# A two-layer hybrid decoder trunk on one core: the instruction order of the scheduler's timeline simulation in place of that of its default model

## The chip, the cores and the metric

The kernel runs on one core of a Trainium2 chip. A core has a matrix engine (TensorE, in the rows PE for the multiplications and PEld for the loading of weights), a vector engine (VectorE, DVE), a scalar engine (ScalarE, ACT), a general engine (GpSimd, POOL) and a queue processor that issues most transfers (SyncE, SP). Each engine runs its own list of instructions in the order in which the program holds them; semaphores order the lists against each other. The metric is the device time of one execution in microseconds, the median of several.

## The reference

The reference is a decoder trunk of two layers on 1024 positions of width 1024, in float32. Cut to what matters:

```python
for i in range(DEPTH):                                  # DEPTH = 2
    proj = rmsnorm(h, attn_norm_g[i]) @ w_in[i]         # one projection, split in ten parts
    y_a = mla_group(c_q, c_kv, k_rope, positions, ...)  # latent attention, rotary key
    y_b = fox_group(fox_qkv, fox_f, fox_b_f[i])         # attention with forget gates
    y_c = hgrn2_group(hg_q, hg_f, hg_i, lb_all[i])      # gated linear recurrence
    y_d = s5_group(s5_u, lam, step, b, c, d, w_glu, ..) # complex diagonal scan, then a GLU
    y = concatenate([rmsnorm(y_a), rmsnorm(y_b), rmsnorm(y_c) * sigmoid(hg_g), rmsnorm(y_d)])
    h = h + y @ w_out[i]
    h = h + conv_ffn(rmsnorm(h, ...), w_up[i], conv_w[i], conv_b[i], w_down[i])  # width 2816, conv of 3
    h = h + sigmoid(rmsnorm(h, ...) @ w_ple_gate[i]) * (p[i] @ w_ple[i])
return rmsnorm(h, final_norm_g)
```

Each of the four groups has 256 of the 1024 columns: four heads of 64 in `mla_group`, `fox_group` and `hgrn2_group`, sixteen blocks of 16 channels with 64 complex states in `s5_group`.

## The kernel before

Activations lie with the features on the 128 partitions and the positions along the row, in halves of 512 positions (tag `h`, 72 buffers). Every float32 product is made as three products of a rounded part and a rest: lines 732 to 734 (`mm3`) and 744 to 746 (`mm3_steps`) issue hi·hi, lo·hi and hi·lo for each block of 128 features. A weight therefore comes in three steps, in `wload`: a DMA on the SP queue into `wr` (2 buffers), a cast to the high part on VectorE (line 720, `wx<-wr`), and the rest on GpSimd or another engine (line 103, `wx<-wr,wx`). `wx` has 6 buffers, so three weights with their two parts; a cast must wait until the products with the weight that had the buffers before are done. PSUM is cut into pools of banks (`pf`, `px`, `po`).

A layer runs in stages that the program writes one after the other, the parts of a stage interleaved by `weave` (a table `T` says at which share of the projection each part begins and ends):

- In-projection, S5 and the recurrence (66 to about 420 us in layer 0, 1583 to 1945 in layer 1). `proj` makes `pj` tiles (24 products each for one half of the positions), `proj_tok` the token-major `ptk`. In the rows `pj<-xs,wx 128*68` is the projection `misc` (68 columns: the rotary key and the forget gates); VectorE takes it out of PSUM at line 1643. Beside it run `s5_mats` (matrices `bare`, `baim` on VectorE and `care`, `caim` on GpSimd, by `cmul`, lines 399 to 404: a complex product of 128x128 tiles is six instructions) and `s5_core` for the two halves of the S5 channels: scans `s5z` on VectorE (lines 591 to 615), 48 products `ys` (lines 625 and 628) on TensorE, transposes `yf` (line 641). `s5_glu` then has the products `gl`. The recurrence has `khT`, `psc`, `poh` on TensorE and `kh`, `qz` on VectorE and GpSimd.
- Attention (420 to 744, 1945 to 2260): logits `lg` and `qk`, maxima `pm`, values `po`, woven with the output projection `ob` of the groups that are done; VectorE adds each `ob` tile into the residual `h` (lines 1765 and 1788).
- FFN up (744 to 1185, 2260 to 2710), FFN down (1185 to 1455, 2710 to 2930; `dn` at lines 1521 to 1523), the gated input embedding (`pg`), and at the very end the final norm.

At the start of a layer's use of a norm, `ss` (line 804) sums squares by a product with ones, and the factor of the norm is then made on ScalarE (lines 810 and 811).

The order of the instructions on each engine is not that of the program text. The framework's scheduler walks through all recorded instructions and lays, engine by engine, the recorded instruction with the best priority (the earliest in the text) that its model of the machine takes to be ready: operands written, a buffer of the pool free. That order is then fixed; the same walk gives out the buffers of each pool. The scheduler is switched on where `kernel` opens the context, at line 2007; all work is written in `body`.

## Time and profile before

| | us |
|---|---|
| median of 3 runs | 3096.61 |
| lowest, highest of them | 3095.42, 3107.64 |
| the profiled execution's own time | 3083.79 |
| its span in the trace | 3082.1 |
| TensorE busy in the span | 2798.3 (91%) |
| VectorE busy | 2521.0 (82%) |
| ScalarE, GpSimd busy | 1403.3, 1228.8 |

The profiled execution is 12.8 us under the median of the runs; its span leaves 1.7 us around it. The rows further down are all of this one execution. Times are from the span's start. [...]

### The profile page before, as it was taken

To read this page: it belongs to the slowest core of one execution; us is meant where nothing else is said; L and a number is where in the kernel's file an instruction comes from. 1 tells how busy PE (TensorE), PEld (TensorE's weight loads), DVE (VectorE), ACT (ScalarE), POOL (GpSimd) and SP (SyncE) were. 2 spreads that over 40 slices of the span, in tenths; PEclk is the share of its full clock that TensorE was granted. 3 is DMA by queue.
4 is the path that set the end of the run, shared out by engine and by line. 5 is a ranking of instruction groups with operands and counts; after the bars stand their busy time and mean duration, and the time that the engine had idled before them with its cause. 6 is when DMAs were issued, how large, how long until landed. Compare 5 with 4: busy or idle time off the path is not lost. (4 is left out here: it accounts for less than half of the span.)

```text
span 3082.1 us, 37399 instructions
## 1 busy us (share of the span) xinstructions
PE 2798.3 (91%) x13082; PEld 2229.8 (72%) x13082; DVE 2521.0 (82%) x3572; ACT 1403.3 (46%) x2448; POOL 1228.8 (40%) x1108
## 2 busy tenths in 40 slices
PE   8889898898999999888999888988989999998897
PEld 6767676676788887666887766766767888876766
DVE  7596878769999998888855877878699999979987
ACT  3124445765444443335722353657654444423355
POOL 3653423445422223555544434324453222245554
PEclk9889999899999999999998989999999999999998
DMA  3101021004122225632511010210032222255423
GB/s 124 37 15 35 20 73 60 9 1 151 67 87 87 83 83 174 202 102 79 161 65 35 18 35 21 79 55 1 35 123 82 83 82 82 78 194 176 134 84 127
DMA packets 124812, 249.70 MB, mean 81 GB/s; under 512 B 18896, under 2 KB 21584, under 8 KB 124624
## 3 DMA queue, kind: packets, MB, share of 16 engines
q1 hardware_dynamic: 123184, 246.66, 23.8%
q8 instruction: 103, 1.69, 0.2%
q10 hardware_dynamic: 1440, 0.65, 0.1%
q14 instruction: 85, 0.70, 0.1%
HBM read 197.58 MB, written 48.50 MB: 80 GB/s over the span
## 5 line engine op out<-in xcount | busy, mean ns | idle before, releaser
L103 POOL TENSOR_TENSOR wx<-wr,wx 128x512 fp32r<-128x512 f32 (+1 forms) x200 | 412.1, 2061 | 433.9 <-DVE wx L720 106.1
L1324 PE MATMUL up<-bh,wx 128*128 128x512 f32 x1232 | 483.2, 392 | 12.1 <-ACT wx L1317 12.1
L1325 PE MATMUL up<-bl,wx 128*128 128x512 f32 x1232 | 483.3, 392 | 6.8 <-DVE bl L103 4.0
L1326 PE MATMUL up<-bh,wx 128*128 128x512 f32 x1232 | 483.6, 392 | 6.3 <-DVE wx L103 6.3
L1523 PE MATMUL dn<-g,wx 128*128 128x512 f32 x616 | 252.3, 410 | 49.9 <-POOL wx L103 25.3
L103 POOL TENSOR_TENSOR pl<-pr,ph 128x512 fp32r<-128x512 f32 x144 | 166.2, 1167 | 308.4 <-ACT pr L980 198.1
L1324 PEld LDWEIGHTS up<-bh,wx 128*128 128x128 f32 x1232 | 233.6, 190 | 62.0 <-ACT wx L1317 13.0
L1325 PEld LDWEIGHTS up<-bl,wx 128*128 128x128 f32 x1232 | 233.9, 190 | 57.3 <-DVE bl L103 4.9
L1326 PEld LDWEIGHTS up<-bh,wx 128*128 128x128 f32 x1232 | 233.3, 189 | 56.7 <-DVE wx L103 8.4
L103 POOL TENSOR_TENSOR wx<-wq,wx 128x512 fp32r<-128x512 f32 x44 | 65.1, 1479 | 517.5 <-ACT wx L1317 517.5
L1521 PE MATMUL dn<-g,wx 128*128 128x512 f32 x616 | 249.7, 405 | 15.6 <-ACT p L1532 11.8
L1522 PE MATMUL dn<-g,wx 128*128 128x512 f32 x616 | 248.8, 404 | 6.0 <-DVE g L103 6.0
L744 PE MATMUL pj<-xs,wx 128*128 128x512 f32 (+1 forms) x512 | 213.0, 416 | 18.9 <-ACT xs L771 7.2
L746 PE MATMUL pj<-xs,wx 128*128 128x512 f32 (+1 forms) x512 | 206.7, 404 | 4.7 <-POOL wx L103 4.2
L745 PE MATMUL pj<-xs,wx 128*128 128x512 f32 (+1 forms) x512 | 208.1, 406 | 0.9 <-DVE xs L772 0.9
L1523 PEld LDWEIGHTS dn<-g,wx 128*128 128x128 f32 x616 | 121.0, 196 | 88.0 <-DVE wx L103 31.6
L1440 ACT CAST g<-g 128x512 fp32r<-128x512 f32 x154 | 92.4, 619 | 154.2 <-DVE g L1463 51.7
L1521 PEld LDWEIGHTS dn<-g,wx 128*128 128x128 f32 x616 | 121.1, 197 | 45.3 <-ACT p L1532 12.6
L1335 DVE SCALAR_TENSOR_TENSOR cv<-u,vec,cv 128x1023 f32<-128x1023 f32 x88 | 131.1, 1491 | 25.5 <-ACT cv L1334 25.2
L1522 PEld LDWEIGHTS dn<-g,wx 128*128 128x128 f32 x616 | 120.9, 196 | 32.9 <-DVE g L103 6.8
L1334 ACT ACTIVATE cv<-u,vec 128x1024 f32<-128x1024 f32 x88 | 109.6, 1245 | 71.7 <-DVE u L1349 46.5
L1336 DVE SCALAR_TENSOR_TENSOR cv<-u,vec,cv 128x1022 f32<-128x1022 f32 x88 | 139.1, 1583 | 0.1
(493 smaller groups left out, 7481.0 us busy)
## 6 DMA issues: line engine op xcount, KB each, us to landing
wr<-in_w_down SPq DMA_DIRECT2D x132, 256.0 KB, 3.1
wr<-in_w_up SPq DMA_DIRECT2D x88, 256.0 KB, 2.9
wq<-in_w_up SPq DMA_DIRECT2D x88, 256.0 KB, 3.8
hid<-cv SPq DMA_DIRECT2D x44, 512.0 KB, 3.0
g<-hid SPq DMA_DIRECT2D x88, 256.0 KB, 5.0
wr<-in_w_fm SPq DMA_DIRECT2D x30, 512.0 KB, 3.7
wr<-in_w_pg SPq DMA_DIRECT2D x28, 512.0 KB, 3.6
hdr<-h SPq DMA_DIRECT2D x48, 256.0 KB, 2.0
```

What stands on the lines that cost most here:

```text
L103: eng.tensor_tensor(out, x, hi.bitcast(F32), op=ALU.subtract)
L744: nc.tensor.matmul(out, lhsT=ah, rhs=bh, start=(i == 0), stop=False)
L745: nc.tensor.matmul(out, lhsT=ah, rhs=bl, start=False, stop=False)
L746: nc.tensor.matmul(out, lhsT=al, rhs=bh, start=False, stop=(i == n - 1))
L1324: nc.tensor.matmul(ps, lhsT=ah, rhs=bh, start=k == 0, stop=False)
L1325: nc.tensor.matmul(ps, lhsT=ah, rhs=bl, start=False, stop=False)
L1326: nc.tensor.matmul(ps, lhsT=al, rhs=bh, start=False, stop=k == KD // 2 - 1)
L1335: V.scalar_tensor_tensor(c[:, 1:], u[:, :S - 1], cw[:, 1:2], c[:, 1:], op0=ALU.mult, op1=ALU.add)
L1336: V.scalar_tensor_tensor(c[:, 2:], u[:, :S - 2], cw[:, 0:1], c[:, 2:], op0=ALU.mult, op1=ALU.add)
L1521: nc.tensor.matmul(o, lhsT=ah, rhs=gh, start=f == 0, stop=False)
L1522: nc.tensor.matmul(o, lhsT=ah, rhs=gl, start=False, stop=False)
L1523: nc.tensor.matmul(o, lhsT=al, rhs=gh, start=False, stop=f == H - 1)
```

## The change

```diff
@@ -2004,7 +2004,7 @@
-    with tile.TileContext(nc) as tc:
+    with tile.TileContext(nc, schedule_with_timeline_sim=True) as tc:
         body(tc, *args, out)
```

The keyword gives the scheduler another model to walk by: one that also simulates how the engines and the other shared devices of a core contend, in place of the default one. No operation, tile, size or engine assignment is changed; every instruction of before is there again by name. What changes is the order on each engine, the buffers that follow from it, and the semaphore waits.

On TensorE the FFN up stage stands as before (the same rows at the same places), as does most of the rest behind the attention; in FFN down the third product of a block (line 1523) stands up to 14 rows further back, behind the first two products of the next tiles. The large moves are in the in-projection and attention stages. At three places they read as follows; the number behind a name is the tile's.

TensorE, layer 0, first half of the S5 channels (`ys_1301`, `ys_1302`) and `misc` (`pj_1341`): before, the last `ys` rows and what follows them.

```order
L628 MATMUL ys_1301<-care_779,s5z_1241 128x128
L628 MATMUL ys_1301<-caim_780,s5z_1242 128x128
L625 MATMUL ys_1302<-tz_989,ut_1197 128x128
L628 MATMUL ys_1302<-care_779,s5z_1241 128x128
L628 MATMUL ys_1302<-caim_780,s5z_1242 128x128
L744 MATMUL pj_1341<-xs_114,wx_1337 68x512
L745 MATMUL pj_1341<-xs_114,wx_1337 68x512
L746 MATMUL pj_1341<-xs_114,wx_1338 68x512
```

After, the last rows of the second half of `misc` (`pj_1415`), the first of the next projection (`pj_1506`, a part of the fox queries), and the `ys` rows that come between them.

```order
L744 MATMUL pj_1415<-xs_174,wx_1337 68x512
L745 MATMUL pj_1415<-xs_175,wx_1337 68x512
L746 MATMUL pj_1415<-xs_174,wx_1338 68x512
L744 MATMUL pj_1506<-xs_114,wx_1502 128x512
L745 MATMUL pj_1506<-xs_114,wx_1502 128x512
L746 MATMUL pj_1506<-xs_114,wx_1503 128x512
L628 MATMUL ys_1301<-care_779,s5z_1241 128x128
L628 MATMUL ys_1302<-care_779,s5z_1241 128x128
L744 MATMUL pj_1506<-xs_117,wx_1502 128x512
L745 MATMUL pj_1506<-xs_117,wx_1502 128x512
```

All but two of the 48 `ys` rows have gone behind the 48 rows of `misc`; the projection `fq` runs between and behind them. The same happens in layer 1 (`pj_13909` and `pj_13983` before `ys_13869`).

VectorE at the same place: the S5 scan (lines 610 to 615), the casts of weights (line 720), `misc` (line 1643) and the first of the 24 instructions that make `bare` and `baim`. Before:

```order
L612 TENSOR_TENSOR s5z_1242<-s5z_1238,phr_1087 128x4x127
L613 TENSOR_TENSOR s5z_1241<-s5z_1241,s5z_1240 128x4x127
L615 TENSOR_TENSOR s5z_1242<-s5z_1242,s5z_1239 128x4x127
L720 CAST wx_1717<-wr_1715 128x1024
L1642 TENSOR_TENSOR hq_1200<-pj_1275,rs_340 128x512
L1643 TENSOR_TENSOR misc_1333<-pj_1341,rs_256 68x512
L399 TENSOR_TENSOR s5t_1387<-bb_764,s5v_728 128x128
L400 TENSOR_TENSOR s5t_1388<-bb_764,s5v_728 128x128
```

After:

```order
L610 TENSOR_TENSOR s5z_1241<-s5z_1239,phr_1087 128x4x127
L612 TENSOR_TENSOR s5z_1242<-s5z_1238,phr_1087 128x4x127
L613 TENSOR_TENSOR s5z_1241<-s5z_1241,s5z_1240 128x4x127
L615 TENSOR_TENSOR s5z_1242<-s5z_1242,s5z_1239 128x4x127
L720 CAST wx_1977<-wr_1975 128x1024
L1643 TENSOR_TENSOR misc_1333<-pj_1341,rs_256 68x512
L399 TENSOR_TENSOR s5t_1387<-bb_764,s5v_728 128x128
L400 TENSOR_TENSOR s5t_1388<-bb_764,s5v_728 128x128
```

`misc` stands behind the same scan. The cast `wx_1717` has gone in front of the scan (row 229 of VectorE's list instead of 248) and `wx_1977` has come in front of `misc` (239 instead of 278). Further on two more casts are early: `wx_1983` at row 259 instead of 333, and the weight of the GLU, `wx_2425`, at row 286 instead of 454. The scans of the second half of the S5 channels, in turn, stand 25 to 29 rows further back.

TensorE, layer 0, where the second half of the S5 channels is transposed (`yf_2231`, `yf_2238`), before: the token-major projection (`ptk_2143`, `ptk_2255`) around it.

```order
L733 MATMUL ptk_2143<-wx_1984,xs_135 128x256
L734 MATMUL ptk_2143<-wx_1983,xs_135 128x256
L641 MATMUL yf_2231<-ident,yt_2137 128x128 x4
L641 MATMUL yf_2238<-ident,yt_2138 128x128 x4
L330 MATMUL psc_2245<-qz_2087,g_2082 128x2x64 x4
L732 MATMUL ptk_2255<-wx_1977,xs_142 128x256
L733 MATMUL ptk_2255<-wx_1978,xs_142 128x256
L734 MATMUL ptk_2255<-wx_1977,xs_143 128x256
```

After:

```order
L628 MATMUL ys_2112<-care_1385,s5z_1924 128x128
L628 MATMUL ys_2112<-caim_1386,s5z_1925 128x128
L641 MATMUL yf_2231<-ident,yt_2137 128x128 x4
L641 MATMUL yf_2238<-ident,yt_2138 128x128 x4
L330 MATMUL psc_2245<-qz_2087,g_2082 128x2x64 x4
L330 MATMUL psc_2310<-qz_2106,g_2101 128x2x64 x4
L330 MATMUL psc_2320<-qz_2180,g_2175 128x2x64 x4
L330 MATMUL psc_2384<-qz_2197,g_2192 128x2x64 x4
```

The 48 `ys` rows of the second half stand some 140 to 170 rows further back, directly ahead of `yf`. The 96 `ptk` rows and the 24 rows of the projection `pj_2537` that stood between `yf` and the end of `gl` now stand ahead of `yf`; behind it only `psc`, `poh`, `gl` and 24 rows of `pj_2679` are left, of which 9 stood there before. By the next chunk of the recurrence (`khT_2702`) both orders have done the same set.

At the start of the attention stage the first `ob` row group (`ob_3518`) now stands ahead of the sum of squares `ss_3370`, and VectorE's addition of it (line 1788) ahead of the four instructions of lines 829 and 831 that wait for that norm; 48 `ob` rows instead of 34 stand ahead of the first `lg`, more of them among the next `lg` rows, and the first `pm` (`pm_3626`) stands 60 rows further back. At the program's start the first `ss` stands behind 14 more rows of `pj`.

## Rows read from the trace of the kernel before

**Rows 1.** The page: the span, and the engines' busy time in it.
```profile
span 3082.1 us, 37399 instructions
PE 2798.3 (91%) x13082; PEld 2229.8 (72%) x13082; DVE 2521.0 (82%) x3572; ACT 1403.3 (46%) x2448; POOL 1228.8 (40%) x1108
```
**Rows 2.** Windows of both layers' attention, busy time: PE, PEld, DVE, ACT, POOL, clock, DMA.
```profile
420.00:560.00 140.00, 128.22 (x598) 95.71 (x598) 112.10 (x206) 85.11 (x167) 41.04 (x45) 0.94 0.13 42
560.00:744.00 184.00, 164.36 (x779) 125.09 (x779) 139.28 (x228) 121.84 (x244) 90.75 (x88) 0.96 0.14 50
1945.00:2260.00 315.00, 281.48 (x1334) 211.48 (x1334) 241.73 (x418) 201.38 (x399) 125.87 (x129) 0.96 0.12 41
```
**Rows 3.** Waits of VectorE, whole span: total us, times, longest.
```profile
DVE misc L1643 <- PE pj L746: 41.4, 2, 20.9
```
**Rows 4.** Timeline of VectorE behind that wait, layer 0: start, duration, idle before.
```profile
153.32 0.69 DVE L1643 TENSOR_TENSOR misc<-pj,rs 68x512 f32<-68x512 f32 x1 [20.54 <-PE pj L746]
153.93 0.28 DVE L399 TENSOR_TENSOR s5t<-bb,s5v 128x128 f32<-128x128 f32 x1
```
**Rows 5.** Windows on both sides of the end of that wait.
```profile
128.00:154.00 26.00, 23.02 (x83) 16.33 (x83) 5.46 (x7) 5.12 (x11) 15.13 (x29) 0.67 0.10 31
154.00:222.00 68.00, 53.73 (x364) 45.17 (x363) 65.28 (x174) 19.00 (x43) 32.00 (x53) 0.93 0.06 17
```
**Rows 6.** Waits of TensorE in 60 to 420: one.
```profile
PE ys L628 <- DVE s5z L613: 3.0, 1, 3.0
```
**Rows 7.** Windows of `ys` alone (PE, PEld, ACT, clock): layer 0, layer 1.
```profile
131.00:145.50 14.50, 14.46 (x46) 10.97 (x46) 0.65 (x2) 0.50 0.13 40
1741.70:1749.40 7.70, 7.67 (x48) 5.92 (x48) 0.65 (x2) 1.00 0.01 2
```
**Rows 8.** Groups of VectorE by shape, 78 to 93: busy us, mean ns.
```profile
L403 DVE TENSOR_TENSOR s5t<-bb,s5v 128x128 f32<-128x128 f32 x4 | 2.0, 492 | 0.0
L402 DVE TENSOR_TENSOR s5t<-bb,s5v 128x128 f32<-128x128 f32 x4 | 1.5, 369 | 0.0
```
**Rows 9.** Window of that stretch (all engines), and timeline of GpSimd during VectorE's wait.
```profile
78.00:93.00 15.00, 8.52 (x71) 8.11 (x69) 13.59 (x43) 1.89 (x5) 12.50 (x32) 0.90 0.02 5
...
135.70 0.41 POOL L400 TENSOR_TENSOR s5t<-prm,s5v 128x128 f32<-128x128 f32 x1
```
**Rows 10.** Windows: `yf` to `gl` (all engines), then `ptk` alone and `pj` alone.
```profile
247.40:291.40 44.00, 41.57 (x259) 33.56 (x258) 28.19 (x37) 21.58 (x39) 13.89 (x8) 0.96 0.11 37
...
261.10:264.20 3.10, 3.03 (x24) 2.94 (x24) 0.43 (x2) 1.00 0.00 0
...
123.80:127.60 3.80, 3.80 (x18) 3.00 (x16) 0.68 (x1) 1.00 0.29 116
```
**Rows 11.** Timeline of TensorE at the start of attention, layer 0.
```profile
409.06 1.12 PE L804 MATMUL ss<-sq,ones 128*128 128x512 f32 x2 [1.08 <-DVE sq L796]
...
417.30 0.39 PE L734 MATMUL ob<-yh,wx 128*128 128x512 f32 x1
420.37 0.50 PE L732 MATMUL ob<-yh,wx 128*128 128x512 f32 x1 [2.68 <-DVE ckv L1642]
```
**Rows 12.** Timeline of VectorE there: the first step behind the norm.
```profile
411.61 0.75 DVE L829 SCALAR_TENSOR_TENSOR xn<-yc,vec,rs 128x512 f32<-128x512 f32 x1 [2.60 <-ACT rs L811]
```
**Rows 13.** Timeline of TensorE at the program's start.
```profile
35.59 2.08 PE L804 MATMUL ss<-sq,ones 128*128 128x512 f32 x2 [4.45 <-DVE sq L796]
```
**Rows 14.** Waits of TensorE in FFN down of layer 0, 1185 to 1455.
```profile
PE dn L1523 <- DVE wx L103: 15.8, 11, 3.1
PE dn L1523 <- POOL wx L103: 10.8, 5, 3.3
```
**Rows 15.** Window in FFN down, layer 0.
```profile
1253.00:1322.00 69.00, 54.83 (x218) 43.09 (x219) 66.32 (x69) 25.45 (x47) 37.32 (x24) 0.93 0.52 169
```

## The prediction

> **What bounds the kernel now.** I read the page first. TensorE is busy 2798.3 of 3082.1 us and VectorE 2521.0 [rows 1]: TensorE leads nearly everywhere, and VectorE is close behind it. No operation changes, so the 283.8 us in which TensorE is idle, and the time that it runs at the lower clock level, are all that another order can win; what it can lose has no such limit. The FFN up stage, where both orders are the same, is out of it. That leaves the in-projection stage, attention, FFN down and the start.
>
> Second came the waits of VectorE. One stands out: its instruction for `misc` waits for the `pj` product 41.4 us in two times, once in each layer, 20.9 at the longest, so 20.5 and 20.9 [rows 3]. The timeline shows why it matters: behind the wait stand instructions of 0.28 us each whose operands have long been there [rows 4]; they are stuck behind `misc` in VectorE's fixed list. The windows on both sides say who pays. During the wait TensorE works 23.0 of 26.0 us, so nothing is lost yet. Behind it, from 154 to 222, VectorE is busy 65.3 of 68.0 us and TensorE only 53.7 [rows 5]: VectorE sets the pace there, and TensorE's idle 14.3 us are what the earlier wait cost. Third, the windows of attention: TensorE idles 11.8 and 19.6 us in layer 0 and 33.5 in layer 1 [rows 2]. Last, the waits in FFN down: 26.6 us of layer 0 stand ahead of line 1523 alone [rows 14].
>
> **The change part by part.** Each term is for both layers, against the profiled execution.
>
> A, the start. The first sum of squares goes behind 14 more `pj` products, so the idle 4.45 us ahead of it [rows 13] is filled. VectorE's square, for which it waited, is no faster, and the norm is then later for whoever needs it. All of it and the slow clock behind it would be 6 us, nothing 0; I take -3.
>
> B, `misc` ahead of `ys`. In the new order `misc` needs no `ys` done, so VectorE's 20.5 and 20.9 us go. Three things take from them. First, the 24 instructions that stood behind the wait had VectorE to themselves (0.28 us each, [rows 4]), because GpSimd did its own such chain during the wait, at 0.41 us each [rows 9]. Now the two chains run side by side. What that costs is seen at 78 to 93, where GpSimd is busy 12.5 of 15.0 us [rows 9] and the same instructions take 0.37 to 0.49 us [rows 8]; with the middle, 0.43, they cost 24 x 0.15 = 3.6 us a layer. The lead is then 16.9 and 17.3 us.
> [...]
> Second, casts of weights come ahead of work: `wx_1977`, `wx_1983` and the GLU's `wx_2425` stand 39, 74 and 168 rows earlier, and a cast that finds its buffer still in use holds all of VectorE. Third, the second half of S5 goes back: its scans by 25 to 29 rows and its `ys` by 140 to 170. So I keep half of the lead: 8.5 + 8.5, B = -17. Checked from TensorE's side: the 3.0 us ahead of `ys` [rows 6] would be filled, and the 48 `ys` run at the clock 0.50 in 14.5 us in layer 0 and at 1.00 in 7.7 us in the other case shown [rows 7]; at the high level they save some 7 us a layer. That is 10 a layer, of the same size, and is bounded by the 14.3 us of idle behind. The ends: all 41.4 kept, -41; and a loss of 28, which is the second rival's price.
>
> C, start of attention. The pair of sums of squares ran from 409.06, the first step behind it on VectorE began at 411.61, 2.6 later [rows 11, 12]. Now its second half stands behind the 12 `ob` products whose last starts at 417.30, so the first step comes at 417.5 + 2.6 = 420.1, and the four steps and a rest at 0.7 each end at 423.6. The next block of `ob` needs them and began at 420.37: 3.2 us later, or 6.5 in two layers. I take +7; none if other work covers it, +12 if the idle lowers the clock behind it.
>
> D, attention. `ob` products move ahead of `lg` and `pm`. TensorE's idle there is 31.4 us in layer 0 and 33.5 in layer 1 [rows 2], in short waits for maxima and probabilities; filling them is what `ob` is there for, and both orders have the same amount of it. I take an eighth of the 65 us, -8. The ends: -20, about a third; and +13 if the 60 `ob` products by which the first `pm` stands further back, at 0.211 us as for `pj` [rows 10], are missed later.
>
> E, FFN down. The third product moves behind the next tiles' first two, which fills waits for the weight's rest: 26.6 us in layer 0 [rows 14]. Where VectorE is busy 66.3 of 69.0 us [rows 15] filling wins nothing, since the weight's rest is itself made there. I take a quarter of what is left of 53 us over both layers when that stretch's share (about half) is gone: -7. The ends: -26 and +4.
>
> The sum is -3 - 17 + 7 - 8 - 7 = -28: the profiled execution's 3083.8 would be 3055.8. It lies 12.8 us under the median of the runs, so the prediction on the median is 3096.6 - 28 = 3069.
>
> **The rivals.** First, no change. VectorE is busy 96% of the stretch behind the wait [rows 5], and a list whose total work is the same gives a lead back wherever a cast holds it. Then B is -6, the rest cancels (C against A and E), and the time is about 3091. For it: the three early casts. Against: the lead of 17 us is larger than any one hold I can find.
>
> Second, slower, because the filling work is spent too early. Between `yf` and the end of `gl` TensorE was busy 41.6 of 44.0 us [rows 10], with 96 `ptk` products (3.03/24 = 0.126 each, 12.1 us) and 24 of `pj_2537` (3.80/18 = 0.211, 5.1 us) that now stand ahead, against 15 more of `pj_2679` (3.2 us): 14.0 us of filling are gone. What is left is the chain from `yf` over `psc` and `poh` to `gl`, which passes VectorE and ScalarE at every step and can't be shortened by order. If it paced those 44 us, TensorE idles 14.0 us a layer, term B becomes +28, and with A and C as above and nothing from D and E the time is 3096.6 - 3 + 28 + 7 = 3129. For it: `ys` goes back directly ahead of `yf`, so `yf` may come no earlier than its 246.4. Against: VectorE is busy only 28.2 of the 44.0 us [rows 10], so filling and not the chain seems to have paced them. It decides when `yf` comes less than half of those 14 us earlier.
>
> Third, a large gain: the wait's whole 41 us are kept, C is covered, A gives 3, D 8 and E 12: 3096.6 - 64 = 3033. For it: TensorE's idle exceeds that many times over. Against: the 14.3 us of idle behind the wait [rows 5] are fewer than 20.5 in layer 0.
>
> That the keyword does nothing is excluded: the lists differ at all three places.
>
> **How the numbers follow.** My forecast has 0.44, no change 0.23, the slower case 0.20, the large gain 0.13. Some 0.5%, 15.5 us, is what a measurement of this kernel tells from no change. The forecast's own range is 3052 to 3086, so a ninth of it lies above 3081 and counts as no change; no change spreads over both limits a little. Faster: 0.39 + 0.13 + 0.02 = 0.54; same: 0.05 + 0.19 + 0.02 = 0.26; slower: 0.20. The range reaches to the large gain's 3033 and up to 3120, short of the slower case's 3129, whose nearer half it takes in.
>
> **What would show it.** Right: VectorE's wait ahead of `misc` is gone or below 5 us in both layers, the 24 instructions behind it take over 0.35 us, most `ys` run at clock 1.00, and the in-projection stage of each layer ends 5 to 12 us earlier relative to its start. C shows as an idle of 4 to 6 us ahead of the second `ob` block. The no-change case shows as new long waits of line 720 on TensorE; the slower one as idle of TensorE of over 10 us between `yf` and the end of `gl`. I am wrong in mechanism if the in-projection stages don't shorten while attention or FFN down move by more than 20 us, and wrong in sign if the idle that goes in one place returns behind the next early cast.

## The result, and the profile after

The changed kernel is slower: 3134.2 us in the median of 4 runs, against 3100.6 for the kernel before on the same chip; the ratio is 1.0104, 95% interval 1.0078 to 1.0130. The forecast was 3069 with a range up to 3120; the second rival's 3129 lies next to the result, but its mechanism, as will be seen, is not what happened.

The profiled execution of the changed kernel took 3133.6 us, its span is 3131.9. That is 49.8 us over the span that the prediction used. A second profile of the kernel before, taken later (e8 below), has a span of 3095.2 and lies at the median of its runs; the first was 13.1 us faster, 6.9 of them in the 64 `poh` products of layer 1 alone (see the last section). Against the second profile the change costs 36.7 us; the medians differ by 33.6. Losses and gains are therefore counted against the second profile. In the in-projection of layer 1, where the two profiles of one order differ by that much, a figure of a few us is spread.

The page after, its first two lines (span; busy time of each engine):

```profile
span 3131.9 us, 37447 instructions
PE 2815.0 (90%) x13082; PEld 2236.7 (71%) x13082; DVE 2465.6 (79%) x3572; ACT 1391.5 (44%) x2448; POOL 1378.0 (44%) x1108
```

Against [rows 1] VectorE is busy 55 us less and GpSimd 149 us more with the same instructions. TensorE is busy 17 us more than in the first profile, but only 1.2 us more than in the second, whose line is:

```profile
PE 2813.8 (91%) x13082; PEld 2240.3 (72%) x13082; DVE 2519.7 (81%) x3572; ACT 1402.6 (45%) x2448; POOL 1228.1 (40%) x1108
```

So the two executions of one order differ in TensorE's busy time (granted clock 0.953 and 0.946 over the span), and the change does not: its clock is 0.945. What the change costs is idle time of TensorE, 316.9 us in place of 281.4 in the second profile: 35.5 of the 36.7 us.

The waits of VectorE, whole span (total us, times, longest):

```profile
DVE wx L720 <- PE pj L745: 107.2, 20, 23.4
DVE h L1765 <- PE ob L734: 39.7, 34, 3.6
```

The wait ahead of `misc` [rows 3] has left the list. In its place the casts of weights wait for TensorE's products, 107.2 us in 20 times. In the two profiles of before the same wait was 57.5 and 66.2 us, in 11 times each.

Where the time went, by the start of the same product in both traces. Each figure is the length of a stretch minus its length in the second profile of before, in us; the four experiments are described below.

| stretch | after | e9 casts | e10 end of attention | e12 three places | e11 best |
|---|---|---|---|---|---|
| start to the end of `pj_1207` (125 us) | -13.0 | -12.3 | -12.8 | -12.2 | -12.0 |
| to `khT_1631` (184) | +11.1 | -2.8 | +11.1 | -2.8 | -2.5 |
| to `khT_2702` (325) | +3.4 | +6.5 | +3.6 | +2.9 | -7.8 |
| to the first `ob` (418) | +8.6 | +7.2 | +8.6 | -1.1 | +0.5 |
| attention, layer 0 (757) | +15.0 | +21.7 | +2.6 | +2.7 | -0.7 |
| FFN up, FFN down (1452) | -8.8 | -9.7 | -8.0 | -8.8 | -7.5 |
| embedding gate, start of layer 1 (1598) | +6.8 | +5.4 | +5.4 | +7.2 | -0.8 |
| in-projection, layer 1 (1950) | +0.1 | -3.5 | -0.5 | -0.9 | +0.5 |
| attention, layer 1 (2293) | +12.5 | +17.9 | +3.1 | +2.2 | -3.3 |
| FFN, layer 1 (2983) | -5.8 | -4.3 | -6.0 | -4.4 | -2.3 |
| embedding gate, final norm (3095) | +6.7 | +6.7 | +6.7 | +7.1 | +3.9 |
| sum | +36.6 | +32.8 | +13.8 | -8.1 | -32.0 |

So the changed kernel leads by 13 us after an eighth of layer 0's work, has lost nearly all of it 60 us later, and loses most in attention, where the prediction expected a gain. FFN gains 14.6 us.

The timeline of VectorE in the changed kernel where [rows 4] was read (start, duration, idle before and what ended it):

```profile
133.07 0.68 DVE L720 CAST wx<-wr 128x1024 fp32r<-128x1024 f32 x1
133.67 0.68 DVE L1643 TENSOR_TENSOR misc<-pj,rs 68x512 f32<-68x512 f32 x1
134.28 0.27 DVE L399 TENSOR_TENSOR s5t<-bb,s5v 128x128 f32<-128x128 f32 x1
...
138.30 0.89 DVE L404 TENSOR_TENSOR baim<-s5t,s5t 128x128 f32<-128x128 f32 x4
151.24 0.69 DVE L720 CAST wx<-wr 128x1024 fp32r<-128x1024 f32 x1 [12.04 <-PE pj L745]
151.85 0.20 DVE L510 TENSOR_TENSOR s5t<-id,dsk 32x64 f32<-32x64 f32 x1
151.98 0.67 DVE L1643 TENSOR_TENSOR misc<-pj,rs 68x512 f32<-68x512 f32 x1
```

`misc` runs at 133.67 without a wait, 19.6 us earlier than in [rows 4] (22.4 earlier than in the second profile), and the 24 instructions follow at once. Then VectorE stands still for 12.04 us: the cast `wx_1983` is next in its list, and its buffer is still read by the products of `pj_1579`, the last of which starts at 151.04. The second half of `misc`, whose products were done at 131.9, stands two places behind that cast and waits with it.

GpSimd in the same stretch:

```profile
123.03 2.41 POOL L103 TENSOR_TENSOR wx<-wr,wx 128x1024 fp32r<-128x1024 f32 x1 [1.62 <-issue]
...
133.89 7.54 POOL L103 TENSOR_TENSOR wx<-wr,wx 128x1024 fp32r<-128x1024 f32 x1 [1.88 <-issue]
```

The same instruction takes 2.41 us and then 7.54 us, just while VectorE makes its 24 products of two operands.

The 48 `ys` of layer 0 that ran at the low level in [rows 7], granted clock 0.50, now run at the high one, 1.00. Window of most of them (length, busy time of PE, PEld and ACT with their instructions, granted clock of TensorE, share of the DMA engines, GB/s):

```profile
134.00:146.40 12.40, 6.53 (x40) 4.89 (x36) 1.29 (x4) 1.00 0.09 22
```

The end of attention in layer 0, timeline of TensorE and then of VectorE in the changed kernel:

```profile
749.76 0.39 PE L734 MATMUL ob<-yh,wx 128*128 128x512 f32 x1
757.52 2.04 PE L804 MATMUL ss<-sq,ones 128*128 128x512 f32 x2 [7.37 <-DVE sq L796]
```

```profile
749.43 1.38 DVE L720 CAST wx<-wr 128x1024 fp32r<-128x1024 f32 x1
750.73 0.68 DVE L1765 TENSOR_TENSOR h<-h,ob 128x512 f32<-128x512 f32 x1
751.33 1.78 DVE L103 TENSOR_TENSOR wx<-wr,wx 128x1024 fp32r<-128x1024 f32 x1
753.04 1.75 DVE L784 TENSOR_TENSOR sq<-sq,sq 128x512 f32<-128x512 f32 x1
754.71 2.06 DVE L1205 SCALAR_TENSOR_TENSOR xq<-h,vec,rs 128x512 f32<-128x512 f32 x3
756.69 0.68 DVE L796 TENSOR_TENSOR sq<-sq,sq 128x512 f32<-128x512 f32 x1
```

TensorE waits 7.37 us for the last sum of squares of the norm. Its operand is the square of line 796, and ahead of that VectorE makes both parts of a weight and three operands of FFN up, none of which is needed yet. In the second profile of before the same place reads (TensorE, then VectorE):

```profile
724.61 0.39 PE L734 MATMUL ob<-yh,wx 128*128 128x512 f32 x1
...
732.14 1.10 PE L804 MATMUL ss<-sq,ones 128*128 128x512 f32 x2 [1.70 <-ACT bh L1224]
```

```profile
724.28 1.38 DVE L720 CAST wx<-wr 128x1024 fp32r<-128x1024 f32 x1
...
727.92 3.48 DVE L1205 SCALAR_TENSOR_TENSOR xq<-h,vec,rs 128x512 f32<-128x512 f32 x2
731.32 0.68 DVE L796 TENSOR_TENSOR sq<-sq,sq 128x512 f32<-128x512 f32 x1
```

There too VectorE makes both parts of a weight and two operands of FFN up ahead of the square, and from the end of the last `ob` to the sum it is 7.1 us, against 7.4 in the changed kernel. The difference is on TensorE: before, 24 `pw` products (the embedding's projection) filled that time; in the new order they have been spent by 746.1, and 5.7 us more of the wait stand open. Layer 1 has the same waits, 7.4 and 1.7 us.

FFN down, waits of TensorE in layer 0, which answer to [rows 14]:

```profile
PE dn L1523 <- DVE wx L103: 20.6, 9, 4.8
PE dn L1523 <- POOL wx L103: 6.4, 3, 3.7
```

27.0 us in place of 26.6 (24.3 in the second profile): the waits that term E wanted to fill are all still there, although the stage is 5.0 us shorter. A wait of 6.1 us ahead of line 1521, in the second profile, is gone.

### The profile page after: what moved, and what is told of

The parts are those of the page before. It is cut to its first block, busy times and chain, and to the rows that moved or that the text cites. A ratio compares the mean times of both kernels' runs of the same rounds, so it can differ in the third digit from the quotient of the medians.

```text
span 3131.9 us, 37447 instructions
## 1 busy us (share of the span) xinstructions
PE 2815.0 (90%) x13082; PEld 2236.7 (71%) x13082; DVE 2465.6 (79%) x3572; ACT 1391.5 (44%) x2448; POOL 1378.0 (44%) x1108
## 5 line engine op out<-in xcount | busy, mean ns | idle before, releaser
L103 POOL TENSOR_TENSOR wx<-wr,wx 128x512 fp32r<-128x512 f32 (+1 forms) x200 | 450.7, 2258 | 420.0 <-DVE wx L720 91.8
L103 POOL TENSOR_TENSOR wx<-wq,wx 128x512 fp32r<-128x512 f32 x44 | 151.8, 3449 | 430.4 <-ACT wx L1317 430.4
L744 PE MATMUL pj<-xs,wx 128*128 128x512 f32 (+1 forms) x512 | 215.0, 420 | 41.7 <-ACT v L1656 11.4
L1523 PE MATMUL dn<-g,wx 128*128 128x512 f32 x616 | 203.8, 410 | 52.3 <-DVE wx L103 41.0
L1521 PE MATMUL dn<-g,wx 128*128 128x512 f32 x616 | 235.4, 406 | 8.0 <-DVE h L1506 4.9
L1522 PE MATMUL dn<-g,wx 128*128 128x512 f32 x616 | 236.8, 403 | 4.8 <-DVE g L103 4.8
L1523 PEld LDWEIGHTS dn<-g,wx 128*128 128x128 f32 x616 | 120.0, 197 | 88.2 <-DVE wx L103 49.3
L720 DVE CAST wx<-wr 128x1024 fp32r<-128x1024 f32 (+1 forms) x72 | 56.2, 784 | 144.1 <-PE pj L745 107.2
L1336 DVE SCALAR_TENSOR_TENSOR cv<-u,vec,cv 128x1022 f32<-128x1022 f32 x88 | 155.9, 1772 | 0.1
L744 PEld LDWEIGHTS pj<-xs,wx 128*128 128x128 f32 (+1 forms) x512 | 100.0, 195 | 70.1 <-ACT v L1656 11.6
L1521 PEld LDWEIGHTS dn<-g,wx 128*128 128x128 f32 x616 | 120.8, 196 | 37.2 <-ACT g L1440 7.0
```

What stands on the lines that cost most here:

```text
L103: eng.tensor_tensor(out, x, hi.bitcast(F32), op=ALU.subtract)
L744: nc.tensor.matmul(out, lhsT=ah, rhs=bh, start=(i == 0), stop=False)
L1336: V.scalar_tensor_tensor(c[:, 2:], u[:, :S - 2], cw[:, 0:1], c[:, 2:], op0=ALU.mult, op1=ALU.add)
L1521: nc.tensor.matmul(o, lhsT=ah, rhs=gh, start=f == 0, stop=False)
L1522: nc.tensor.matmul(o, lhsT=ah, rhs=gl, start=False, stop=False)
L1523: nc.tensor.matmul(o, lhsT=al, rhs=gh, start=False, stop=f == H - 1)
```

## The experiments

All of them take the instructions of the kernel and say only in which order they may be laid. A helper adds, before the scheduler runs, a dependency without a semaphore from each instruction of a list to the one before it:

```diff
+def pin(tc):
+    nc = tc.nc
+    dep = mybir.DependencyInfo(mybir.DependencyClass.NoSync, mybir.DependencyReason.DATA)
+    for line in PINS.strip().splitlines():     # one chain of instruction numbers
+        ...
+            tc.add_manual_dep(i, last, dep, reason="order")
...
         body(tc, *args, out)
+        pin(tc)
```

The lists are made from the two orders, cut at a time of the first profile of before into sets that are closed under dependencies. In the diffs below `a` is the new order and `b` the old, with the end of each stretch in us; `all` are the five engines' lists. Where nothing is said of an engine, the scheduler with the timeline simulation lays it.

**Theory F** was, from the first two traces: filling products are spent too early on TensorE, which then idles and drops to its lower level (in the changed kernel the 64 `poh` of layer 0 ran at the granted clock 0.54). **Rival A**: the reordered attention makes the loss. **Rival B**: VectorE's order in the in-projection does (early casts, late scans).

e1, the in-projection put back on all engines, and e2, its mirror image:

```diff
 e1  all: a to 60, then
+    all: b to 415; a to 1584; b to 1946; a to the end
 e2  all: b to 60, then
+    all: a to 415; b to 1584; a to 1946; b to the end
```

> The changed order everywhere, but in the in-projection stage of both layers every engine has the order of before. Theory F (TensorE's filling products are spent too early there, TensorE then idles and its clock falls): the two stages cost some 13 and 19 us in the profiles, so the time falls by about 30 from 3134 to 3100-3108. Rival A (the reordered attention with ob ahead of lg and pm makes the loss): it stays above 3120.

> The mirror image: the order of before everywhere, but the in-projection stage of both layers in the new order on every engine. Theory F: some 30 us slower than before, 3125-3135. Rival A: within 10 us of before, below 3110.

e1 measured 3114.0 us, ratio to before 1.0058 (1.0038 to 1.0079). e2 measured 3121.7, ratio 1.0094 (1.0070 to 1.0118), on a chip where before ran at 3095.3. Put into the old kernel the new in-projection costs 0.9%; taken out of the new one it gives back 0.5%. The effects don't add up: what a stage loses or wins is partly taken up by the next. Neither theory has its numbers: e1 lies above F's 3108, e2 a little under F's 3125.

e3, attention put back:

```diff
 e3  all: a to 415, then
+    all: b to 745; a to 1946; b to 2270; a to the end
```

> The changed order everywhere, but in the attention stage of both layers every engine has the order of before. Theory F: attention is 5 to 15 us of the loss, so 3119-3129. Rival A: most of the loss goes, 3100-3108.

Measured 3118.0, ratio 1.0081 (1.0054 to 1.0108). Attention is then 1.3 and 1.2 us longer than before, in place of 15.0 and 12.5, but FFN loses some of its gain. A part of the loss, as F said, and not most of it.

e4, in the in-projection TensorE alone put back, and e5, VectorE alone:

```diff
 e4  all: a, but from 60 to 415 and from 1584 to 1946
+    TensorE: b, the others free
 e5  all: a, but from 60 to 415 and from 1584 to 1946
+    VectorE: b, the others free
```

> The changed order, but in the in-projection stage of both layers TensorE alone has the order of before; the other engines are laid by the timeline simulation around it. Theory F: TensorE's order is what costs, so most of what the first of these kernels wins back comes back here too: 3100-3112. Rival B (the early casts of weights and the late scans on VectorE make the loss): less than 10 us come back, 3124-3136.

> The changed order, but in the in-projection stage of both layers VectorE alone has the order of before; the others are laid by the timeline simulation around it. TensorE's order alone, put back, cost another 24 us. Theory F (filling products spent early on TensorE): VectorE's old order beside TensorE's new one leaves the loss, 3125-3140. Rival B (VectorE's early casts and late scans): 15 us or more come back, below 3118.

e4 measured 3152.6, ratio 1.0187 (1.0165 to 1.0208): by the two ratios, 25 us slower than the changed kernel. That is where F fell for this stage: TensorE's old order alone, with the others laid around it, doesn't help, it hurts. In its trace `misc` waits 21.9 us again, since `ys` stands ahead of it. e5 measured 3131.3, ratio 1.0105 (1.0079 to 1.0131), as F expected and against B. But its trace says otherwise of the place: `khT_1631` starts at 169.7 in place of 181.6 and `khT_2702` at 304.8 in place of 326.3, 20 us ahead of the kernel before. Then attention takes 21.5 and 20.8 us more than before. The total alone would have misled; a stage was mended and the next gave it back. In layer 0 the place is the second `ob` block: TensorE waits 9.0 us ahead of it, and 10.2 in layer 1 (see e9).

e6, TensorE's old order in layer 0 alone, from `khT_2702` to attention:

```diff
 e6  all: a, but from 322 to 415
+    TensorE: b, the others a
```

> The changed order on all engines; on TensorE alone, in layer 0 alone, the products from the chunk khT_2702 of the recurrence to the start of attention stand as before, so that pj products stand among psc and poh again. Theory F: the 64 poh products run at the clock 1.00 in some 12 us in place of 18.6 at 0.54, the stretch from khT_2702 to ob_3518 falls from 101.6 to about 94, the time by 5-9 us to about 3126. Rival G (the chain from psc over VectorE to poh sets the stretch, and the products only move): stretch above 99, poh still after an idle.

Measured 3135.1, ratio 1.0118 (1.0095 to 1.0140). Windows of the 64 `poh` alone (length, PE, PEld, ACT, clock), in the first profile of before, in the changed kernel, and in e6:

```profile
377.30:389.30 12.00, 11.59 (x64) 6.06 (x64) 0.59 (x1) 1.00 0.14 45
```

```profile
384.90:403.50 18.60, 18.59 (x64) 8.68 (x64) 0.59 (x1) 0.54 0.00 1
```

```profile
384.00:404.00 20.00, 11.69 (x64) 6.06 (x64) 1.02 (x2) 0.84 0.00 1
```

With `pj` products among them again, the 64 `poh` take 11.69 us of TensorE as before, 7 us less than in the changed kernel. The stretch from `khT_2702` to the first `ob` got no shorter all the same: 105.8 us, against 101.6. What the clock gives back behind the start of `poh_3232` (+0.4 us there in place of +5.5, against before), the way to it takes (+12.4 in place of +3.1): VectorE's list brings the operands of `psc` and `poh` no earlier, and now `pj` products stand in their way. Rival G's number holds (above 99); its idle ahead of `poh` doesn't show, for from 384.0 to 391.4 TensorE is busy 7.29 of 7.40 us, at the granted clock 0.58. The low level costs 6.6 us at `poh` in the changed kernel (18.6 us at 0.54, against 12.0 at 1.00); in e6 it lies ahead of `poh`, and TensorE's order alone does not mend the stretch.

e7, the new order in FFN alone, put into the kernel before, and e8, the kernel before once more for a second profile:

```diff
 e7  all: b to 745, then
+    all: a to 1450; b to 2270; a to 2969; b to the end
```

> The order of before, but FFN up and FFN down of both layers in the new order on every engine. By the profiles these stages gain 8.6 us in layer 0 and 5.4 in layer 1. If that is kept, the time is 10-14 us under before, ratio 0.9955 to 0.9968. Rival H (what FFN down gains, the gated embedding behind it gives back, since it waits for weights that come no earlier): within 5 us of before, ratio above 0.9985.

> The kernel before once more, for a second profile: the one that the prediction used lies 12 us under the median of the runs. Stages that differ between the two by more than 2 us are spread and not an effect of the order.

e7 measured 3089.0, ratio 0.9971 (0.9956 to 0.9985): faster, by 9 us, a little short of the 10 to 14 expected. The gain in FFN is real, and the gated embedding gives nothing back in layer 0 (-0.0 us); in layer 1 the embedding and the final norm take 2.1 us back in its profile. e8 measured 3097.0.

e9, only the casts: each cast of line 720 in the in-projection no earlier than behind the instruction that it followed before; 36 chains of two instructions.

```diff
 e9  all: a, but from 60 to 415 and from 1584 to 1946
+    free, with 36 x (instruction ahead of the cast in b, cast)
```

> The changed order, but in the in-projection stage of both layers each cast of a weight (line 720) on VectorE may not come before the instruction that it follows in the order of before; all else there is laid by the timeline simulation. With VectorE's whole old order there, layer 0 reached khT_1631 at 169.7 in place of 181.6. Theory K (the early casts hold VectorE while their buffers are in use): khT_1631 comes at 168-174 and the first 420 us get 10 or more shorter. Rival S (the S5 scans that stand further back on VectorE): khT_1631 stays above 179.

Measured 3129.7, ratio 1.0112 (1.0088 to 1.0135). Timeline of VectorE in e9, to be held against the changed kernel's:

```profile
128.60 0.68 DVE L720 CAST wx<-wr 128x1024 fp32r<-128x1024 f32 x1
129.20 0.68 DVE L1643 TENSOR_TENSOR misc<-pj,rs 68x512 f32<-68x512 f32 x1
...
139.28 0.69 DVE L1643 TENSOR_TENSOR misc<-pj,rs 68x512 f32<-68x512 f32 x1 [4.42 <-PE pj L746]
...
140.71 0.80 DVE L720 CAST wx<-wr 128x1024 fp32r<-128x1024 f32 x1
```

The second half of `misc` comes 12.7 us earlier and the 12.04 us of standing still are gone. `khT_1631` starts at 168.4: theory K is right at its place, and rival S is wrong there. Behind it the stretch from `khT_1631` to `yf_2231` is 4.7 us longer than before, and 6.4 shorter in e5, which has all of VectorE's old order; that the late scans make the difference is likely but not shown. Of 11.4 us at the first `ob` 4.8 are left at FFN up, and the time is that of the changed kernel. Most of what is lost again goes at one place, the second `ob` block of layer 0, here in e9 and then in the changed kernel:

```profile
429.40 0.80 PE L732 MATMUL ob<-yh,wx 128*128 128x512 f32 x1 [8.96 <-DVE h L1788]
```

```profile
435.26 0.50 PE L732 MATMUL ob<-yh,wx 128*128 128x512 f32 x1 [2.03 <-ACT yh L832]
...
437.12 0.50 PE L733 MATMUL ob<-yl,wx 128*128 128x512 f32 x1 [1.36 <-POOL yl L103]
```

In e9 VectorE lays the steps of lines 829 and 831 and then both parts of a weight ahead of the addition of line 1788 that this block waits for.

e10, the end of attention put back:

```diff
 e10 all: a to 680, then
+    all: b to 765; a to 2205; b to 2290; a to the end
```

> The changed order, but at the end of attention (the work that before did in its last 75 us of it, in both layers) all engines have the order of before. Theory T (the loss in attention comes at its end, where VectorE makes operands of FFN up ahead of the squares that TensorE waits for, and the filling products are gone): 7 to 11 us a layer come back, 3113-3120, ratio 1.004 to 1.006. Rival: the softmax part lost it, and under 8 us in all come back.

Measured 3110.9, ratio 1.0055 (1.0037 to 1.0073): by the ratios 15 us of the 33 come back, from some 85 us of work in each layer. Attention is 2.6 and 3.1 us longer than before, in place of 15.0 and 12.5.

e12, three places at once: the casts as in e9, the old order from `khT_2702` over the start of attention, and the end of attention as in e10:

```diff
 e12 all: a to 60
+    free to 322, casts as in e9; all: b to 445; a to 680; b to 765; a to 1584
+    free to 1846, casts as in e9; all: b to 1975; a to 2205; b to 2290; a to the end
```

> The changed order, but with the three places put back at once, in both layers: the casts of weights of the in-projection no earlier than before, the order of before from khT_2702 over the start of attention to its first 25 us, and the order of before at the end of attention. If these three places are the loss (by the ledgers 10, 14 and 12 us in layer 0, less in layer 1), the time falls below before: 3085-3095, ratio 0.997 to 1.000. If what one place wins is given back at the next, as the casts alone showed, it stays at 3105-3115, ratio 1.003 to 1.006.

Measured 3083.4, ratio 0.9957 (0.9937 to 0.9978), a little better than the 0.997 expected. With these three places put back, the new order is faster than the old one; the whole loss of 1.04% was there. Mended alone, the casts gave nothing in the total, the end of attention 0.5%; together with the stretch from `khT_2702` over the start of attention they give 1.5%. That third place has no run of its own with all engines put back.

e11, the best of both: e5's order in layer 0 up to `khT_2702`, the new order in FFN, the old one elsewhere.

```diff
+e11 all: e5 to 322; b to 745; a to 1450; b to 2270; a to 2969; b to the end
```

> The order of before, but layer 0 up to the chunk khT_2702 in the order of the kernel with VectorE's old order in the in-projection, and FFN up and down of both layers in the new order. By the ledgers 17 us come from the first and 8 to 14 from the second: 22 to 30 us under before, ratio 0.990 to 0.993. If the lead is given back at the end of that stage, 0.996 to 0.998 as with the FFN part alone.

Measured 3062.7, ratio 0.9896 (0.9877 to 0.9915), 31 us under before's 3093.9 on its chip: faster than both kernels. Its page:

```profile
span 3063.4 us, 37448 instructions
PE 2798.3 (91%) x13082; PEld 2230.4 (73%) x13082; DVE 2499.2 (82%) x3572; ACT 1394.7 (46%) x2448; POOL 1360.1 (44%) x1108
```

## Why the prediction was wrong

The terms beside what the table of stretches shows, in us for both layers:

| term | predicted | measured |
|---|---|---|
| A, start | -3 | -1.1 |
| not priced: TensorE's wait for `caim` ahead of `pk` (7.1 us, and the low level behind it: 0.50 from 93.2 to 95.0 in the first profile) | 0 | -11.9 by the end of `pj_1207`, in layer 0 |
| B, `misc` and what follows to the first `ob` | -17 | +23.1 in layer 0, +0.1 in layer 1 |
| C, start of attention (first `ob` to first `lg`) | +7 | +11.9 (5.3 and 6.6) |
| D, attention behind it | -8 | +15.6 (9.7 and 5.9) |
| E, FFN down (first `dn` to first `pg`) | -7 | -5.0 and -2.0 |
| not priced: FFN up | 0 | -3.8 and -3.8 |
| not priced: embedding gates, norms | 0 | +6.8 and +6.7 |

**B, the step that failed first: "So I keep half of the lead".** What came before it was right: the wait of 20.5 us is gone, the 24 instructions start 19.6 us earlier, and `ys` runs at the high level (1.00). Of the three things that take from the lead, the first cost nothing on VectorE (the 24 instructions took 4.9 us in all, as fast as alone; GpSimd paid, see below), and the second cost the most: one early cast held VectorE for 12.04 us. Of the 22.4 us that VectorE leads at `misc`, 9.7 are left at its second half. The prediction named that cast, `wx_1983`, and its 74 places, wrote that the lead of 17 us was larger than any one hold it could find, and gave this hold no price. It could have been priced: the cast takes a buffer that the fox queries' products read, those products stand around and behind `ys` in the new TensorE list, and their end was to be had by adding 7.7 us of `ys` [rows 7] and 24 x 0.211 twice to the end of `misc` (131.9): 149.7, against the 151.2 at which the cast ran. e9 shows the other side: with the casts late (all 36, so this one isn't singled out), `khT_1631` comes 15.1 us earlier than in the second profile of before, so the 12.3 us of lead that TensorE has at the end of `pj_1207` are not only kept but grow. How much of the 15.1 is due to `misc` and how much to the earlier `pk` isn't separated. In layer 1 two casts hold VectorE, 9.59 us ahead of `misc` and 5.59 ahead of its second half: the wait of 20.9 us there has for the most part become a wait of casts.

**D, the sign.** Attention was priced by its mean idle and by an eighth of it. The loss lies before the hand-over to FFN up, and e10 shows it: with the last 85 us in the old order, 12.4 and 9.4 us of it come back. In layer 0, 5.7 of the 12.4 are TensorE's longer wait for the last sum of squares. Here theory F's mechanism is seen in the rows: VectorE is as late in both orders, and the 24 `pw` that would fill the wait are spent. e10 puts all engines back, so it doesn't single this out, and the other 6.7 us aren't traced. The prediction's order rows stopped at attention's start, and this move of the `pw` wasn't priced.

**C** is at the upper end of its bounds, +11.9 for +7, but in part by where the stretch is cut: 48 `ob` stand ahead of the first `lg` in place of 34, and 14 at 0.227 us are 3.2 us a layer that are moved and not lost. That leaves 5.5 for C, and 6.4 more for D. The chain is as told (in layer 0 the sum of squares at 430.63, the first step of line 829 at 433.07), but TensorE's idle ahead of the second `ob` block is 3.4 us against 2.7 before, and not the 4 to 6 that were named as its sign. In e9, where the stage comes earlier, it is 9.0.

**E** came out at its size, -7.0, by luck: the waits of line 1523 that it was to fill are as long as before. e7 shows that a gain of about 9 us is an effect of FFN's own order; which of its moves makes it I haven't separated. FFN up's part lies in its first 115 us: behind them, for 327.4 us, the two traces run in step.

**The rivals.** The second had the right time, 3129, for the wrong reason. Its condition was met, since `yf_2231` started at 248.2 and not earlier than 246.4, and still the stretch from `yf` to `khT_2702` grew by 2.6 us and not by 14, although TensorE ran at the granted clock 0.65 from 249.3 to 274.0 and at 0.73 from there to the end of `gl` at 295.8. In e11 all 96 `ptk` stand ahead of `yf` as well, and the stretch is as long as before (+0.1). So the chain did pace those 44 us, against what the prediction held, and the filling work wasn't lost, since `yf` came no later with it ahead (248.2 in the changed kernel, 227.0 in e11, 249.3 in the second profile of before). The first rival named the mechanism that decided the in-projection of layer 0, and gave it too small a price.

What stays open: what makes the 8.6 us from `khT_2702` to the first `ob` (e6 shows only that TensorE's order alone doesn't mend them); why attention in layer 1 takes back 5.4 us of what e9 wins ahead of it (the 6.5 to 6.7 us in layer 0, and the 8.3 of e5 in layer 1, are for the most part the wait of 9 to 10 us ahead of the second `ob` block); and what lengthens the embedding gates, where in layer 0 GpSimd waits 26.9 us for casts of ScalarE, against 18.0.

## What to carry to other kernels

In a fixed order, an instruction that frees or fills a buffer early is only as harmless as the one that its buffer waits for: for each cast or load that a change moves up, find the last reader of its buffer in the new order and price the hold on everything queued behind it (here one early cast held VectorE for 12.04 us). Look for the losses at the hand-overs between stages, where a chain over other engines must be waited out: what counts there is whether work that fills the wait is still unspent, and a mean over the stage doesn't show it. And judge a repair by the length of its own stretch and of the next before its total: here a stage could be mended by 11 us without the time showing it, and three repairs that gave 0, 0.5% and an unmeasured third alone were worth 1.5% together.

## What the runs showed of the hardware that was not expected

VectorE and GpSimd at work side by side did not share the loss. During VectorE's 24 back-to-back instructions of two operands (134.28 to 139.2) one subtraction on GpSimd took 7.54 us, against 2.41 us 11 us earlier: 5.1 us more, the length of VectorE's run, while VectorE's instructions took 0.27 to 0.28 us as when alone. In layer 1 the same run of VectorE stands beside a subtraction of 7.69 us. The kernel before, with 86 such subtractions in each of its two profiles, has none over 3.06. In the earlier case it was VectorE's instruction that took longer:

```profile
123.42 2.58 DVE L596 TENSOR_TENSOR s5z<-s5z,s5z 128x512 f32<-128x512 f32 x1
```

It began 0.4 us behind GpSimd's subtraction of 123.03 and ended 0.6 behind it, where an addition of this kind takes 0.68 us with GpSimd at rest (line 615 at 132.47). At 78 to 93 in the kernel before, where GpSimd was busy 12.50 of 15.00 us [rows 9], VectorE's instructions of lines 402 and 403 took 0.37 and 0.49 us in the mean [rows 8], and not 0.28 as in [rows 4]. So the loss doesn't fall on the same engine each time, and what decides it isn't shown. The prediction charged it to VectorE, 3.6 us a layer; in this run it cost GpSimd. It isn't shown that this was free: at 158.30 VectorE waits 2.95 us for GpSimd.

The 64 `poh` of layer 0 took 11.59 us at the granted clock 1.00, and 18.59 at 0.54 in the changed kernel. What TensorE did there before its clock fell (all engines: length, PE, PEld, DVE, ACT, POOL, clock):

```profile
357.00:371.00 14.00, 6.80 (x33) 6.37 (x33) 13.75 (x28) 5.45 (x13) 8.03 (x14) 0.70 0.11 39
378.30:386.50 8.20, 6.83 (x53) 5.90 (x52) 6.40 (x11) 2.36 (x4) 0.00 (x0) 1.00 0.00 0
386.50:403.50 17.00, 17.00 (x56) 7.77 (x55) 0.75 (x2) 0.59 (x1) 0.00 (x0) 0.50 0.00 1
```

Up to 371 TensorE waits for VectorE, which is busy 13.75 of 14.00 us. The `pj` products right behind that wait run for the most part at the low level (0.64 from 371.0 to 378.3). Then TensorE is back at the full level (1.00 from 378.3), and falls again at 386.5, to 0.50, in the midst of `poh`, where it works without a pause (17.00 of 17.00 us). So what the 64 `poh` lose doesn't stand right behind the long wait. In layer 0 the level went with the order: the 64 `poh` took 12.0 us in both profiles of before, in e1, e7 and e12, and 18.5 to 18.7 in the changed kernel, e2, e3, e9 and e10. In layer 1 it did not. There the same products in the same order ran at either level in the first and the second profile of the kernel before:

```profile
1903.00:1917.80 14.80, 11.76 (x64) 6.06 (x64) 0.59 (x1) 1.00 0.11 35
1906.50:1928.30 21.80, 16.10 (x64) 7.72 (x64) 0.64 (x2) 0.63 0.08 24
```

That is over half of the 13.1 us between these two executions, and a reason to take a second profile before an effect of a few us is read from one.
